# Where the small products of the norms between sub-layers stand in TensorE's order

## The chip, the cores and the metric

One core of one Trainium2 chip runs the whole program. The metric is the device time of one execution in microseconds; of several executions the median is given.

## What is computed

One inference step of a hybrid backbone: two layers of three sub-layers each, on 512 latent and 128 context tokens of width 1024. A sub-layer is wrapped in two RMS norms:

```python
def rms_norm(x, gain):
    x32 = x.astype(F32)
    y = x32 * lax.rsqrt(jnp.mean(x32 * x32, axis=-1, keepdims=True) + RMS_EPS)
    return y.astype(x.dtype) * gain

def modulated_in(x, gain, m):
    return rms_norm(x, gain) * (1 + m[:, None, 1]) + m[:, None, 0]

def residual_out(x, y, gain, m, weight):
    return x + weight * m[:, None, 2] * rms_norm(y, gain)
```

The input of a sub-layer is `modulated_in(x)`, its output y goes into x by `residual_out`. The sub-layers in order are (0,0) SwiGLU, (0,1) attention together with an RWKV-7 scan, (0,2) SwiGLU, (1,0) SwiGLU, (1,1) a bidirectional S5, (1,2) SwiGLU.

## The kernel before

Everything is kept transposed: 128 channels on the partitions, 640 tokens along the free axis, eight tiles `x[d]` for the 1024 channels. The tokens are worked in two halves of 320 columns, half 0 and half 1. Each weight block of 128 columns is loaded by a DMA (`w`), split by `wsplit` (L402) into a high part `whi` (a cast on ScalarE, ACT) and a low part `wlo` (a subtraction on VectorE, DVE, or now and then on GpSimd, POOL), and the activations are split alike into `hh` and `hl`. A product of a block is `mm3` (L431): for each of the eight (or more) tiles of the contraction three matmuls of 128x320, lines L440, L441 and L442. In what follows "a product" is one call of `mm3`, "a matmul" one instruction.

The last stage of a sub-layer goes through its output blocks for half 0, then for half 1. Each block is copied out (y), squared on ACT (L373) and added up on POOL (ssy, L374). When the last block of a half is out, `on_half` (L2072) is called. It runs this chain, with x in place:

- `rms_bcast` of ssy (L326): three matmuls of one column, `ps_ms` (L333); add of the epsilon on DVE (L336); the power on POOL (`rr`, L337); three `diag` on DVE (L341); three matmuls `ps_rb` that spread the factors over all partitions (L342). `ps_ms` and `ps_rb` are the small products that this document is about.
- `post_norm` (L382): per tile, yr = y times factors on DVE (L391), x += yr on DVE (L394), then the square on ACT (L373) and its add on POOL (`ssx`, L374).
- `rms_bcast` of ssx, and `pre_norm` (L345) for the next sub-layer: xr on DVE (L355), `hh` on ACT (L357), `hl` on DVE (L358).

For half 0 the chain runs while PE works on half 1's blocks. For half 1 the post-norm is emitted at once, with the first weights of the next sub-layer ahead of it (`early_weights`, L416); its second part, from ssx on, is kept in `pending` and emitted by `flush` (L444) after the next sub-layer's first products of half 0, in `ab` at L783, in `s5` at L1889. The next sub-layer does its first blocks for half 0, then the same for half 1, then goes on block by block.

The order on each engine is not the order of the code: a scheduler places the instructions by their dependences, their priorities and an estimate of their times; `issue_after` bars an instruction from standing ahead of another one. Within an engine the order that it wrote is kept on the chip, so that an instruction that waits holds up all that stand behind it on its engine.

Of the kernel before, what the change touches and what calls it, by code (L numbers as in the profile page):

```python
# [17 lines left out]
KT = D // 128  # L18
# [14 lines left out]
class K:  # L33


    def __init__(self, ctx, tc, I, O):
        self.ctx, self.tc, self.nc, self.I, self.O = ctx, tc, tc.nc, I, O
        self.pools, self.last, self.last_load = {}, [None] * 3, None
        self.const = self.open("const", 1)
        self.dram = self.open("dram", 1, space=bass.MemoryType.DRAM)  # L40

# [71 lines left out]
    def setup(self):  # L113
# [107 lines left out]
        for t in range(4):  # L221
            self.ada_piece(0, 0, 1, t, pre[4 + t])
        self.first_norm = self.pre_norm(0, 0, 0, rb)
        self.pending = lambda: self.pre_norm(0, 0, 1, self.rms_bcast(ss))
        self.close("boot")
        self.boot = None

# [96 lines left out]
            self.nc.sync.dma_start(dst, xo)  # L324


    def rms_bcast(self, ss):

        nc = self.nc
        ps = self.ps("ps_ms", "pn")  # L330

        for i, c in enumerate((0, 128, 192)):
            nc.tensor.matmul(ps[:, i:i + 1], ss[:, c:c + 128], self.mean, start=True, stop=True)  # L333
        ms = self.small.tile([128, 4], F32, name="ms")
        r = self.small.tile([128, 4], F32, name="rr")
        nc.vector.tensor_scalar(ms[:, :3], ps[:, :3], 1e-6, None, op0=OP.add)  # L336
        self.last_norm = nc.gpsimd.tensor_tensor(r[:, :3], ms[:, :3], self.mhalf[:, :3], op=OP.pow)  # L337
        rb = self.ps("ps_rb", "pn")
        dg = self.small.tile([128, HALF], F32, name="diag")
        for i, (p, c, n) in enumerate(((0, 0, 128), (0, 128, 128), (64, 256, 64))):  # L340
            nc.vector.tensor_scalar(dg[p:, c:c + n], self.ident[p:, p:], r[p:, i:i + 1], None, op0=OP.mult)  # L341
            nc.tensor.matmul(rb[:, c:c + n], self.ones[p:, :], dg[p:, c:c + n], start=True, stop=True)  # L342
        return rb

    def pre_norm(self, l, j, half, rb):  # L345
# [33 lines left out]
            self.sq_add(ss, self.x[d][:, half * HALF:(half + 1) * HALF], d == 0)  # L379
        return ss  # L380

    def post_norm(self, l, j, half, y, ssy, stats=True):  # L382

        nc = self.nc
        m = self.mods[l, j]
        rb = self.rms_bcast(ssy)
        ss = self.small.tile([128, HALF], F32, name="ssx", bufs=2) if stats else None
        for d in range(KT):
            t = self.small.tile([128, HALF], F32, name="yr", tag="n320", bufs=4)
            for a, b, g in SEGS[half]:  # L390
                nc.vector.scalar_tensor_tensor(t[:, a:b], y[d][half][:, a:b], m[:, 2, d, g:g + 1], rb[:, a:b],  # L391
                                               op0=OP.mult, op1=OP.mult)
            xs = self.x[d][:, half * HALF:(half + 1) * HALF]
            nc.vector.tensor_tensor(xs, xs, t, op=OP.add)  # L394
            if stats:
                self.sq_add(ss, xs, d == 0)
        return ss
# [35 lines left out]
    def mm3(self, ps, whl, acts, half, kt, k0=0, k1=None):  # L433

        nc = self.nc
        hi, lo = whl
        ah, al = acts
        o = ps[:, :HALF]
        for k in range(k0, k1 or kt):
            nc.tensor.matmul(o, hi[:, k], ah[k][half], start=(k == 0), stop=False)  # L440
            nc.tensor.matmul(o, hi[:, k], al[k][half], start=False, stop=False)  # L441
            self.last[0] = nc.tensor.matmul(o, lo[:, k], ah[k][half], start=False, stop=(k == kt - 1))  # L442

    def flush(self):  # L444

        if self.pending:
            with ExitStack() as c:
                for i in self.last:
                    c.enter_context(self.tc.issue_after(i.ins))
                self.pending()  # L450
        self.pending = None


# [276 lines left out]
    def ab(self, l, j, on_half, fillers):  # L730
# [36 lines left out]
        def weights(kind, n, eng=None):  # L767
            if self.early[1]:
                return self.early[1].pop(0)
            if kind == "q":  # L770
                return q_weights(n)
            return in_weights({"rw": 768 + n * 128, "k": 512, "v": 640}[kind], eng)

        def one(item, half, w):
            ps = self.ps("ps_in")
            self.mm3(ps, w, acts, half, KT)
            self.ab_take(*item, half, ps)


        for n in range(ahead):  # L780
            one(seq[n], 0, weights(*seq[n], nc.gpsimd if n in (4, 6) else None))
        nxt = [weights(*seq[n]) for n in range(3)]
        self.flush()  # L783
        self.ab_setup()
        for n in range(ahead):
            one(seq[n], 1, nxt.pop(0) if nxt else weights(*seq[n]))
# [947 lines left out]
    def s5(self, l, j, on_half, fillers):  # L1734
# [150 lines left out]
        for d in range(KT):  # L1885
            if d in (4, 6):
                in_load(d // 2)
            proj(d, 0, in_weights(d))
        self.flush()  # L1889
        ws = []  # L1890
        rows = self.t320("s5_s0r")[:, :128]
        self.load(rows, I["state_s5"][0, 0].rearrange("d r (p h) n -> (d r p) (h n)", h=2))
# [166 lines left out]
    def run(self, subs):  # L2059
# [7 lines left out]
        for n, (l, j) in enumerate(order):  # L2067
# [2 lines left out]
            nxt = order[n + 1] if n + 1 < len(order) else None  # L2070

            def on_half(half, y, ssy):  # L2072
                if half and nxt:
                    self.early_weights(*nxt)
                ss = self.post_norm(l, j, half, y, ssy, nxt is not None)
                if nxt and half == 0:
                    self.new_h()
                    self.pre_norm(*nxt, 0, self.rms_bcast(ss))
                elif nxt:
                    self.pending = lambda to=nxt, ss=ss: self.pre_norm(*to, 1, self.rms_bcast(ss))  # L2080

            fill = ([late] if n == 0 else []) + self.ada(l, j, (2,))
            if nxt:
# [73 lines left out]
```

## Time and profile before

| what | value |
|---|---|
| median of 3 executions | 3195.02 us (3191.65 to 3197.65) |
| the profiled execution | 3184.59 us |
| its span | 3182.8 us |
| PE busy | 2900.1 us (91%), 22675 matmuls |
| DVE, ACT, POOL busy | 2080.4 us (65%), 1267.9 us (40%), 954.2 us (30%) |
| mean granted clock | 0.942 of full speed |

The profile is one execution. PE is TensorE. "Idle before" an instruction is the time in which its engine stood still ahead of it, with what ended that time behind the arrow. The granted clock of a stretch is given as a share of 2.4 GHz. A matmul's length overlaps with its neighbours, so that its cost is read from start to start.

### The profile page before, as it was taken

To read this page: it belongs to the slowest core of one execution; us is meant where nothing else is said; L and a number is where in the kernel's file an instruction comes from. 1 tells how busy PE (TensorE), PEld (TensorE's weight loads), DVE (VectorE), ACT (ScalarE), POOL (GpSimd) and SP (SyncE) were. 2 spreads that over 40 slices of the span, in tenths; PEclk is the share of its full clock that TensorE was granted. 3 is DMA by queue.
4 is the path that set the end of the run, shared out by engine and by line. 5 is a ranking of instruction groups with operands and counts; after the bars stand their busy time and mean duration, and the time that the engine had idled before them with its cause. 6 is when DMAs were issued, how large, how long until landed. Compare 5 with 4: busy or idle time off the path is not lost. (4 is left out here: it accounts for less than half of the span.)

```text
span 3182.8 us, 57458 instructions
## 1 busy us (share of the span) xinstructions
PE 2900.1 (91%) x22675; PEld 2704.9 (85%) x22675; DVE 2080.4 (65%) x4199; ACT 1267.9 (40%) x2675; POOL 954.2 (30%) x1010
## 2 busy tenths in 40 slices
PE   6999998987788788999999999999986689999997
PEld 5999998875566567999999999999985589989997
DVE  4876687524746654864675885665777945976776
ACT  4533345423444434533333552332452235533343
POOL 2322235114312201533241322232223633332332
PEclk8999998987888888999999999999997889999998
DMA  6434325631111107354453455453468753442223
GB/s 248 139 120 133 121 89 189 206 133 49 22 33 31 26 15 204 100 171 130 152 157 118 150 153 164 138 163 105 151 149 213 275 177 113 146 146 83 90 71 116
DMA packets 367411, 412.76 MB, mean 130 GB/s; under 512 B 75433, under 2 KB 332262, under 8 KB 366630
## 3 DMA queue, kind: packets, MB, share of 16 engines
q1 hardware_dynamic: 351270, 359.64, 36.8%
q0 software_dynamic: 15872, 49.45, 5.1%
q8 instruction: 179, 2.93, 0.4%
q14 instruction: 90, 0.74, 0.1%
HBM read 357.74 MB, written 50.10 MB: 128 GB/s over the span
## 5 line engine op out<-in xcount | busy, mean ns | idle before, releaser
L413 DVE TENSOR_TENSOR wlo<-w,whi 128x1024 fp32r<-128x1024 f32 (+3 forms) x486 | 472.4, 979 | 265.0 <-ACT whi L412 259.2
L412 ACT CAST whi<-w 128x1024 fp32r<-128x1024 f32 (+3 forms) x488 | 394.4, 817 | 572.7 <-PE ps_y L441 189.7
L440 PE MATMUL ps_h<-hh,whi 128*128 128x320 f32 x1248 | 390.4, 314 | 4.8 <-ACT hh L357 2.4
L441 PE MATMUL ps_h<-hl,whi 128*128 128x320 f32 x1248 | 390.5, 313 | 0.7 <-DVE hl L358 0.7
L442 PE MATMUL ps_h<-hh,wlo 128*128 128x320 f32 x1248 | 389.0, 312 | 0.1
L442 PE MATMUL ps_y<-gh,wlo 128*128 128x320 f32 x1056 | 327.2, 312 | 1.5 <-DVE wlo L413 1.2
L441 PE MATMUL ps_y<-gl,whi 128*128 128x320 f32 x1056 | 327.5, 312 | 0.0
L440 PE MATMUL ps_y<-gh,whi 128*128 128x320 f32 x1056 | 323.8, 314 | 2.6 <-ACT whi L412 1.4
L440 PEld LDWEIGHTS ps_h<-hh,whi 128*128 128x128 f32 x1248 | 236.5, 190 | 9.0 <-issue 3.0
L441 PEld LDWEIGHTS ps_h<-hl,whi 128*128 128x128 f32 x1248 | 236.2, 189 | 5.4 <-issue 3.5
L442 PEld LDWEIGHTS ps_h<-hh,wlo 128*128 128x128 f32 x1248 | 236.1, 189 | 2.6 <-issue 2.0
L440 PEld LDWEIGHTS ps_y<-gh,whi 128*128 128x128 f32 x1056 | 198.1, 189 | 7.9 <-issue 2.5
L442 PEld LDWEIGHTS ps_y<-gh,wlo 128*128 128x128 f32 x1056 | 199.1, 189 | 4.5 <-DVE wlo L413 2.7
L503 DVE TENSOR_TENSOR wlo<-w,whi 128x512 fp32r<-128x512 f32 x216 | 181.8, 867 | 31.7 <-ACT whi L502 30.8
L441 PEld LDWEIGHTS ps_y<-gl,whi 128*128 128x128 f32 x1056 | 199.6, 189 | 1.7 <-issue 1.3
L502 ACT CAST whi<-w 128x512 fp32r<-128x512 f32 x216 | 128.0, 619 | 154.6 <-POOL w L517 47.6
L440 PE MATMUL ps_wide<-hh,whi 128*128 128x320 f32 x576 | 182.3, 317 | 2.5 <-ACT hh L357 1.3
L441 PE MATMUL ps_wide<-hl,whi 128*128 128x320 f32 x576 | 181.4, 315 | 0.4 <-DVE hl L358 0.4
L442 PE MATMUL ps_wide<-hh,wlo 128*128 128x320 f32 x576 | 180.6, 314 | 0.0
L718 DVE TENSOR_TENSOR y<-y,ps_y 128x320 f32<-128x320 f32 x228 | 108.8, 483 | 88.4 <-PE ps_y L442 87.7
L374 POOL TENSOR_TENSOR ssy<-ssy,sq 128x320 f32<-128x320 f32 x84 | 88.6, 1055 | 204.1 <-ACT sq L373 201.2
L374 POOL TENSOR_TENSOR ssx<-ssx,sq 128x320 f32<-128x320 f32 x84 | 102.7, 1224 | 125.7 <-ACT sq L373 121.9
(583 smaller groups left out, 7864.7 us busy)
## 6 DMA issues: line engine op xcount, KB each, us to landing
w<-in_ffn_w_dram SPq DMA_DIRECT2D x112, 1024.0 KB
ada_w<-in_ada_w_dram SPq DMA_DIRECT2D x72, 1024.0 KB
w<-in_ffn_w_dram SPq DMA_DIRECT2D x104, 512.0 KB
w<-in_ab_w_in_dram SPq DMA_DIRECT2D x14, 1024.0 KB
xd<-x POOLq DMA_DIRECT2D x4, 2560.0 KB, 10.8
s5cd<-s_work POOLq DMA_DIRECT2D x128, 64.0 KB, 2.4
s5bd<-s_st POOLq DMA_DIRECT2D x32, 256.0 KB, 4.3
s5bt<-s5bd SPq DMA_DIRECT2D x32, 256.0 KB
```

What stands on the lines that cost most here:

```text
L374: nc.gpsimd.tensor_tensor(ss, ss, sq, op=OP.add)
L412: a = self.nc.scalar.copy(hi[:, :kt], s)
L413: v = (eng or self.nc.vector).tensor_tensor(lo[:, :kt], s, hi[:, :kt].bitcast(F32), op=OP.subtract)
L440: nc.tensor.matmul(o, hi[:, k], ah[k][half], start=(k == 0), stop=False)
L441: nc.tensor.matmul(o, hi[:, k], al[k][half], start=False, stop=False)
L442: self.last[0] = nc.tensor.matmul(o, lo[:, k], ah[k][half], start=False, stop=(k == kt - 1))
L502: nc.scalar.copy(h, src)
L503: v = nc.vector.tensor_tensor(l, src, h.bitcast(F32), op=OP.subtract)
L718: nc.vector.tensor_tensor(yt, yt, ps[:, :HALF], op=OP.add)
```

## The change

`rms_bcast` is cut in two, `rms_stat` (from ps_ms to rr) and `rms_rows` (diag and ps_rb). Half 0's chain is no longer emitted at once: `later(n, step)` puts a step on a list, and `tick`, called at the end of each product, counts down and emits it, with `issue_after` that product's last matmul. So of half 1's eight products the second is followed by ps_ms of ssy, the third by ps_rb and the post-norm, the seventh by ps_ms of ssx, the eighth by ps_rb and the pre-norm. Of half 1's chain the post-norm's small products are held: manual dependences put ps_ms behind the first and ps_rb behind the second product of the next sub-layer. `flush` emits only ps_ms of ssx, and ps_rb with the pre-norm comes one product later; in `ab` and `s5` the call of `flush` goes one product forward for that. The number of instructions on each engine stays as it was, and SP's queue, which issues the loads, keeps its order.

```diff
--- before.py
+++ after.py
@@ -36,6 +36,8 @@
     def __init__(self, ctx, tc, I, O):
         self.ctx, self.tc, self.nc, self.I, self.O = ctx, tc, tc.nc, I, O
         self.pools, self.last, self.last_load = {}, [None] * 3, None
+
+        self.todo, self.hold, self.pending = [], [], None
         self.const = self.open("const", 1)
         self.dram = self.open("dram", 1, space=bass.MemoryType.DRAM)
 
@@ -221,7 +223,7 @@
         for t in range(4):
             self.ada_piece(0, 0, 1, t, pre[4 + t])
         self.first_norm = self.pre_norm(0, 0, 0, rb)
-        self.pending = lambda: self.pre_norm(0, 0, 1, self.rms_bcast(ss))
+        self.pending = ss, lambda rb: self.pre_norm(0, 0, 1, rb)
         self.close("boot")
         self.boot = None
 
@@ -324,22 +326,54 @@
             self.nc.sync.dma_start(dst, xo)
 
 
+    def later(self, n, step):
+
+        self.todo.append([n, step])
+
+    def tick(self):
+
+        for i in self.hold.pop(0) if self.hold else ():
+            self.tc.add_manual_dep(
+                i, self.last[0].ins.name,
+                mybir.DependencyInfo(mybir.DependencyClass.NoSync, mybir.DependencyReason.DATA),
+                reason="norm behind a product")
+        if self.todo:
+            self.todo[0][0] -= 1
+            if self.todo[0][0] <= 0:
+                with self.tc.issue_after(self.last[0].ins):
+                    self.todo.pop(0)[1]()
+
+    def drain(self):
+        while self.todo:
+            self.todo.pop(0)[1]()
+
     def rms_bcast(self, ss):
+        return self.rms_rows(self.rms_stat(ss))
+
+    def rms_stat(self, ss):
 
         nc = self.nc
         ps = self.ps("ps_ms", "pn")
+        self.small_products = [[], []]
 
         for i, c in enumerate((0, 128, 192)):
-            nc.tensor.matmul(ps[:, i:i + 1], ss[:, c:c + 128], self.mean, start=True, stop=True)
+            self.small_products[0].append(
+                nc.tensor.matmul(ps[:, i:i + 1], ss[:, c:c + 128], self.mean, start=True, stop=True).ins)
         ms = self.small.tile([128, 4], F32, name="ms")
         r = self.small.tile([128, 4], F32, name="rr")
         nc.vector.tensor_scalar(ms[:, :3], ps[:, :3], 1e-6, None, op0=OP.add)
         self.last_norm = nc.gpsimd.tensor_tensor(r[:, :3], ms[:, :3], self.mhalf[:, :3], op=OP.pow)
+        return r
+
+    def rms_rows(self, r):
+
+        nc = self.nc
         rb = self.ps("ps_rb", "pn")
         dg = self.small.tile([128, HALF], F32, name="diag")
         for i, (p, c, n) in enumerate(((0, 0, 128), (0, 128, 128), (64, 256, 64))):
             nc.vector.tensor_scalar(dg[p:, c:c + n], self.ident[p:, p:], r[p:, i:i + 1], None, op0=OP.mult)
-            nc.tensor.matmul(rb[:, c:c + n], self.ones[p:, :], dg[p:, c:c + n], start=True, stop=True)
+            self.small_products[1].append(
+                nc.tensor.matmul(rb[:, c:c + n], self.ones[p:, :], dg[p:, c:c + n], start=True, stop=True).ins)
         return rb
 
     def pre_norm(self, l, j, half, rb):
@@ -379,11 +413,10 @@
             self.sq_add(ss, self.x[d][:, half * HALF:(half + 1) * HALF], d == 0)
         return ss
 
-    def post_norm(self, l, j, half, y, ssy, stats=True):
+    def post_norm(self, l, j, half, y, rb, stats=True):
 
         nc = self.nc
         m = self.mods[l, j]
-        rb = self.rms_bcast(ssy)
         ss = self.small.tile([128, HALF], F32, name="ssx", bufs=2) if stats else None
         for d in range(KT):
             t = self.small.tile([128, HALF], F32, name="yr", tag="n320", bufs=4)
@@ -440,6 +473,8 @@
             nc.tensor.matmul(o, hi[:, k], ah[k][half], start=(k == 0), stop=False)
             nc.tensor.matmul(o, hi[:, k], al[k][half], start=False, stop=False)
             self.last[0] = nc.tensor.matmul(o, lo[:, k], ah[k][half], start=False, stop=(k == kt - 1))
+        if (k1 or kt) == kt:
+            self.tick()
 
     def flush(self):
 
@@ -447,7 +482,9 @@
             with ExitStack() as c:
                 for i in self.last:
                     c.enter_context(self.tc.issue_after(i.ins))
-                self.pending()
+                ss, norm = self.pending
+                stat = self.rms_stat(ss)
+            self.later(1, lambda: norm(self.rms_rows(stat)))
         self.pending = None
 
 
@@ -779,8 +816,10 @@
 
         for n in range(ahead):
             one(seq[n], 0, weights(*seq[n], nc.gpsimd if n in (4, 6) else None))
+            if n == ahead - 2:
+                self.flush()
+        self.drain()
         nxt = [weights(*seq[n]) for n in range(3)]
-        self.flush()
         self.ab_setup()
         for n in range(ahead):
             one(seq[n], 1, nxt.pop(0) if nxt else weights(*seq[n]))
@@ -1886,7 +1925,9 @@
             if d in (4, 6):
                 in_load(d // 2)
             proj(d, 0, in_weights(d))
-        self.flush()
+            if d == KT - 2:
+                self.flush()
+        self.drain()
         ws = []
         rows = self.t320("s5_s0r")[:, :128]
         self.load(rows, I["state_s5"][0, 0].rearrange("d r (p h) n -> (d r p) (h n)", h=2))
@@ -2070,14 +2111,30 @@
             nxt = order[n + 1] if n + 1 < len(order) else None
 
             def on_half(half, y, ssy):
-                if half and nxt:
-                    self.early_weights(*nxt)
-                ss = self.post_norm(l, j, half, y, ssy, nxt is not None)
-                if nxt and half == 0:
+                if half:
+
+                    self.drain()
+                    if nxt:
+                        self.early_weights(*nxt)
+                    ss = self.post_norm(l, j, 1, y, self.rms_bcast(ssy), nxt is not None)
+                    if nxt:
+                        self.hold = self.small_products
+                        self.pending = ss, lambda rb, to=nxt: self.pre_norm(*to, 1, rb)
+                    return
+                box = {}
+
+                def post():
+                    box["ss"] = self.post_norm(l, j, 0, y, self.rms_rows(box["r"]), nxt is not None)
+
+                def pre():
                     self.new_h()
-                    self.pre_norm(*nxt, 0, self.rms_bcast(ss))
-                elif nxt:
-                    self.pending = lambda to=nxt, ss=ss: self.pre_norm(*to, 1, self.rms_bcast(ss))
+                    self.pre_norm(*nxt, 0, self.rms_rows(box["s"]))
+
+                self.later(2, lambda: box.update(r=self.rms_stat(ssy)))
+                self.later(1, post)
+                if nxt:
+                    self.later(4, lambda: box.update(s=self.rms_stat(box["ss"])))
+                    self.later(1, pre)
 
             fill = ([late] if n == 0 else []) + self.ada(l, j, (2,))
             if nxt:
```

The order on PE from the end of (0,0) on. Here ps_wide<-gh is the last product of (0,0), ssx and ssy are the sums of squares (ssy_4908 is half 1's), ps_in and ps_wide<-hh are products of (0,1), hh_0 of half 0 and hh_1 of half 1. Before:

```order
L442 MATMUL ps_wide<-gh,wlo 128x320
L333 MATMUL ps_ms<-mean,ssx 128x1 x3
L342 MATMUL ps_rb<-diag,ones 128x128 x2
L342 MATMUL ps_rb<-diag,ones 128x64
L333 MATMUL ps_ms<-mean,ssy_4908 128x1 x3
L440 MATMUL ps_in<-hh_0_5378,whi 128x320 x3
...
L342 MATMUL ps_rb<-diag,ones 128x128 x2
L342 MATMUL ps_rb<-diag,ones 128x64
...
L333 MATMUL ps_ms<-mean,ssx 128x1 x3
L342 MATMUL ps_rb<-diag,ones 128x128 x2
L342 MATMUL ps_rb<-diag,ones 128x64
L440 MATMUL ps_wide<-hh_1_5379,whi 128x320
```

And with the change:

```order
L475 MATMUL ps_wide<-gh,wlo 128x320
L361 MATMUL ps_ms<-mean,ssx 128x1 x3
L376 MATMUL ps_rb<-diag,ones 128x128 x2
L376 MATMUL ps_rb<-diag,ones 128x64
L473 MATMUL ps_in<-hh_0_5602,whi 128x320 x3
...
L361 MATMUL ps_ms<-mean,ssy_4908 128x1 x3
...
L376 MATMUL ps_rb<-diag,ones 128x128 x2
L376 MATMUL ps_rb<-diag,ones 128x64
...
L361 MATMUL ps_ms<-mean,ssx 128x1 x3
...
L376 MATMUL ps_rb<-diag,ones 128x128 x2
L376 MATMUL ps_rb<-diag,ones 128x64
L473 MATMUL ps_wide<-hh_1_5603,whi 128x320
```

The three products of ssy_4908 moved from ahead of the first product of (0,1) to 52 matmuls later; ps_rb moved from 32 matmuls after the start of half 0 to 82; ps_ms of ssx moved from directly ahead of the next ps_rb to one product (24 matmuls) ahead of it. So 62 matmuls stand between ps_rb and ps_ms of ssx, where 136 stood.

The order on DVE at (0,2) to (1,0): diag and xr belong to half 1's pre-norm, hl_1_18622 and hl_1_18889 are its first tile's low part, s_work is background work for the later S5. Before:

```order
L341 TENSOR_SCALAR diag<-ident,rr 64x64
L413 TENSOR_TENSOR wlo<-w,whi 128x512 x2
...
L1694 TENSOR_TENSOR s_work<-s_bc,s_lp 128x2x16x8
L1695 TENSOR_TENSOR s_work<-s_bc,s_lp 128x2x16x8
L355 SCALAR_TENSOR_TENSOR xr<-x,mods_13285,ps_rb 128x192
...
L355 SCALAR_TENSOR_TENSOR xr<-x,mods_13285,ps_rb 128x128
L413 TENSOR_TENSOR wlo<-w,whi 128x1024
L1678 TENSOR_TENSOR s_work<-s_work 128x256 x2
L1696 TENSOR_TENSOR s_work<-s_work 128x256
L358 SCALAR_TENSOR_TENSOR hl_1_18622<-xr,mods_13285,hh_1_18606 128x192
```

And with the change:

```order
L374 TENSOR_SCALAR diag<-ident,rr 64x64
L446 TENSOR_TENSOR wlo<-w,whi 128x512
L446 TENSOR_TENSOR wlo<-w,whi 128x1024
L389 SCALAR_TENSOR_TENSOR xr<-x,mods_13285,ps_rb 128x192
...
L389 SCALAR_TENSOR_TENSOR xr<-x,mods_13285,ps_rb 128x128
L1715 TENSOR_TENSOR s_work<-s_bc,s_lp 128x256
...
L1734 TENSOR_TENSOR s_work<-s_bc,s_lp 128x2x16x8
L446 TENSOR_TENSOR wlo<-w,whi 128x1024 x2
L392 SCALAR_TENSOR_TENSOR hl_1_18889<-xr,mods_13285,hh_1_18873 128x192
```

Six s_work stood ahead of the first xr, and one wlo and three more s_work between the last of the eight xr and the first hl; now those six stand, with two wlo, between the last xr and the first hl.

Counts of 128x320 matmuls at the other places, read from the same orders:

| place | before | with the change |
|---|---|---|
| (0,0) to (0,1): matmuls by which half 0's first ps_ms is later |  | 36 |
| (0,1) to (0,2): the same |  | 8 to 9 |
| (0,1) to (0,2): from ps_rb of half 1's pre-norm to half 1's first product | 101 | 48 |
| (0,2) to (1,0): the same | 36 | 16 |
| (1,0) to (1,1): matmuls by which half 1's ps_rb of the post-norm is later |  | 14 |
| (1,1) to (1,2): matmuls by which half 0's ps_rb of the post-norm is later |  | 11 |
| (1,1) to (1,2): the same | 80 | 36 |

On POOL at the end of (0,0), four adds of half 1's ssy stood between half 0's last ssx add and the power of its pre-norm; with the change one stands ahead of the ssx adds and two behind them.

## Rows read from the trace of the kernel before

**Rows 1.** Waits of PE, whole span: total us, times, longest.

```profile
PE ps_rb L342 <- DVE diag L341: 20.7, 7, 6.0
PE ps_ms L333 <- POOL ssy L374: 11.7, 4, 3.9
PE ps_ms L333 <- POOL ssx L374: 6.8, 3, 3.9
```

**Rows 2.** Windows: length, busy us (count) of PE, PEld, DVE, ACT, POOL, granted clock, DMA.

```profile
491.40:498.20 6.80, 5.42 (x20) 5.14 (x21) 3.67 (x7) 3.13 (x4) 2.12 (x3) 0.50 1.01 322
sum 90.40, PE 63.51 PEld 58.23 DVE 63.31 ACT 32.42 POOL 20.97; mean PE 7.06 PEld 6.47 DVE 7.03 ACT 3.60 POOL 2.33
```

**Rows 3.** PE's timeline, end of (0,0): start, length, instruction, [idle before it <- releaser].

```profile
492.78 1.44 PE L333 MATMUL ps_ms<-mean,ssy 128*128 128x1 f32 x6 [3.92 <-POOL ssy L374]
494.19 0.64 PE L440 MATMUL ps_y<-gh,whi 128*128 128x320 f32 x1
495.89 0.47 PE L440 MATMUL ps_y<-gh,whi 128*128 128x320 f32 x1
...
498.02 0.40 PE L442 MATMUL ps_y<-gh,wlo 128*128 128x320 f32 x1
...
501.46 0.31 PE L442 MATMUL ps_y<-gh,wlo 128*128 128x320 f32 x1
...
502.93 0.31 PE L440 MATMUL ps_y<-gh,whi 128*128 128x320 f32 x1
```

**Rows 4.** ACT's timeline, end of (0,0) and of the last sub-layer.

```profile
493.30 1.56 ACT L412 CAST whi<-w 128x768 fp32r<-128x768 f32 x2 [2.88 <-DMA w<-in_ffn_w_dram]
...
3135.01 1.56 ACT L412 CAST whi<-w 128x768 fp32r<-128x768 f32 x2 [4.24 <-DMA w<-in_ffn_w_dram]
```

**Rows 5.** PE's timeline, (0,1) to (0,2), and (1,1) to (1,2).

```profile
1263.74 1.01 PE L333 MATMUL ps_ms<-mean,ssy 128*128 128x1 f32 x4 [3.18 <-POOL ssy L374]
...
1295.30 1.81 PE L342 MATMUL ps_rb<-diag,ones 128*128 128x128 f32 x6 [3.98 <-DVE diag L341]
...
2694.53 1.84 PE L342 MATMUL ps_rb<-diag,ones 128*128 128x128 f32 x6 [3.78 <-DVE diag L341]
```

**Rows 6.** PE's timeline, start of (0,1).

```profile
525.06 1.81 PE L342 MATMUL ps_rb<-diag,ones 128*128 128x128 f32 x6 [6.00 <-DVE diag L341]
534.90 0.97 PE L342 MATMUL ps_rb<-diag,ones 128*128 128x128 f32 x6
...
557.35 0.83 PE L333 MATMUL ps_ms<-mean,ssx 128*128 128x1 f32 x6 [1.35 <-POOL ssx L374]
```

**Rows 7.** DVE's timeline in the last sub-layer: the last x of half 0.

```profile
3153.32 1.16 DVE L394 TENSOR_TENSOR x<-x,yr 128x320 f32<-128x320 f32 x1
```

**Rows 8.** POOL's lines, 539.4 to 557.4 us: total and mean ns | idle before.

```profile
L374 POOL TENSOR_TENSOR ssx<-ssx,sq 128x320 f32<-128x320 f32 x7 | 11.9, 1698 | 0.3
L413 POOL TENSOR_TENSOR wlo<-w,whi 128x1024 fp32r<-128x1024 f32 x2 | 5.2, 2606 | 8.4 <-ACT whi L412 8.4
L301 POOL DMA_DIRECT2D xd<-x x1 | 0.6, 612 | 0.0
```

**Rows 9.** PE's timeline, (0,2) to (1,0).

```profile
1847.09 0.43 PE L342 MATMUL ps_rb<-diag,ones 64*128 64x64 f32 x2
1854.14 0.41 PE L440 MATMUL ps_wide<-hh,whi 128*128 128x320 f32 x1 [1.12 <-ACT y L716]
1855.08 0.41 PE L441 MATMUL ps_h<-hl,whi 128*128 128x320 f32 x1 [0.31 <-DVE hl L358]
```

**Rows 10.** DVE's timeline, (0,2) to (1,0).

```profile
1847.04 0.42 DVE L1676 TENSOR_TENSOR s_work<-s_bc,s_lp 128x256 f32<-128x256 f32 x1 [0.41 <-DMA s_bc<-s5bc]
...
1849.88 2.41 DVE L355 SCALAR_TENSOR_TENSOR xr<-x,mods,ps_rb 128x192 f32<-128x192 f32 x8
1852.19 1.23 DVE L413 TENSOR_TENSOR wlo<-w,whi 128x1024 fp32r<-128x1024 f32 x1
```

**Rows 11.** PE's timeline, (1,0) to (1,1).

```profile
2359.25 1.44 PE L333 MATMUL ps_ms<-mean,ssx 128*128 128x1 f32 x6 [3.90 <-POOL ssx L374]
```

## The prediction

> **What bounds the kernel now.** TensorE (PE) is the busiest engine by far (the table above), so time is won only where PE stands still or is clocked down. I read its waits first: ps_rb behind the DVE's diag 20.7 us, ps_ms behind POOL's ssy adds 11.7, ps_ms behind its ssx adds 6.8 [rows 1]; together 39.2 us. Then the granted clock of the stretches behind these waits: nine of them, 90.4 us in all, at 0.50, that is 1.2 GHz, with PE busy for 63.5 us [rows 2]. One matmul of 128x320 takes 0.267 us there (eight from 495.89 to 498.02) and 0.147 at 2.4 GHz (ten from 501.46 to 502.93 [rows 3]), so at most half of the 63.5 us, 32 us, lies in the clock. The upper bound of the whole idea is thus 39 + 32 = 71 us. The question is which of these waits end on something that the change moves.
>
> **What goes at the first wait of a boundary.** At (0,0) to (0,1) PE idles 3.92 us for ssy and issues its next real product at 494.19 [rows 3]. That product needs a whi, whose cast ACT starts at 493.30, after a wait for the DMA of w_ffn; two casts take 1.56 us, so the first is done near 494.1 [rows 4]. With the small product out of the way PE would have idled until the same 494.19. The end of the last sub-layer reads alike: ACT waits 4.24 us for a DMA there and starts the cast at 3135.01 [rows 4]. SP's queue keeps its order, so both are costed at 0 gained; were the load earlier, 3.9 each would be won. At (0,1) to (0,2) the ssy wait is 3.18 us [rows 5]; nine matmuls more ahead of it fill 9 x 0.147 = 1.3 of it. But half 0's chain (yr, x, eight squares, seven adds on POOL, pow, diag) starts no earlier, and it sets the later wait of 3.98 us [rows 5]: I take -1.2 (-2.5 to +1).
>
> **What is late next, half 0.** Elsewhere a chain starts later. In (0,0) to (0,1) ps_ms goes 36 matmuls back: from 494.19, at half clock until 498.2, they end near 501.3, and with 33 more ps_rb stands near 506, where it is soon after 500 now. Six us later start yr and x. The second ps_rb has waited 6.00 us until 525.06 [rows 6]. In POOL's old order four adds of the other half stood ahead of this chain's pow; now three do. I cost it at +1.2 (0 if the chain has all the slack, +3 if half of the six arrives). At (1,1) to (1,2) the rows part moves 11 matmuls = 1.6 us back, and the 3.78 us wait [rows 5] hangs on that chain: +1.6 (0 to +3). At the end x of half 0 was complete at 3154.5 [rows 7], and comes about 6 later, near the time at which PE reads it: +0.5 (0 to +1.5).
>
> **Half 1, whose post-norm is now held behind the next sub-layer's products.** This is the larger part.
> (a) (0,0) to (0,1): ps_ms of ssy goes 52 matmuls back. PE starts on ps_in at 526.9 without it, 20 matmuls at half clock until 532.3 and 65 at full, so ps_rb moves from 534.90 to 542. ps_ms of ssx, though, stands 24 matmuls *earlier* than before, since flush went one product forward: 62 matmuls lie between the two, 136 before. From ps_rb to ssx it took 557.35 - 534.90 = 22.4 us, of which PE waited 1.35 [rows 6]. POOL was full for the last 18: seven adds 11.9, two wlo 5.2, a spill 0.6 [rows 8]. In the new order the two wlo stand together ahead of the adds, which I take to save some 7 us of the 22.4, their own 5.2 and some waiting for squares; so the last add is still at about 557.5, while PE arrives at 542 + 0.9 + 62 x 0.147 = 552. A new wait of 5 to 6 us, then 24 matmuls at half clock (6.4 us) ahead of ps_rb, which were done by then before: ps_rb at 564.8 for 561.08. Half 1 starts 2 to 6.5 us later: +3.5.
> A page speaks against this place too. The Trainium skill (SBUF — State Buffer, section Who interferes with whom) says that a DVE instruction with two SBUF inputs and a GpSimd one that reads SBUF exclude each other. The seven adds took 1.70 us each [rows 8], and wlo and x += yr on the DVE are of that kind. By that rule each add that newly meets a wlo could lose up to the DVE's 1.2 us; the sum goes by the row, which holds such meetings already.
> (b) (0,1) to (0,2): 48 matmuls are left between ps_rb and half 1, before 101. 48 x 0.147 = 7.1 us cover the xr, hh and hl work of the first tiles with little to spare: +1 (0 to +2).
> (c) (0,2) to (1,0): 16 matmuls are left, before 36: 2.4 us of cover. Before, ps_rb's last product started at 1847.09, PE got its first hl at 1855.08, and waited 1.12 and 0.31 us [rows 9]. In the new DVE order eight xr, six s_work and two wlo stand in between: 2.4 + 6 x 0.4 + 2 x 1.2 = 7.2 us [rows 10]. So the first hl is about 7.5 us behind ps_rb, when PE has 2.4 us of ps_y and 0.6 of hh products to do. A new wait of 4 to 5 us, and, as behind the 3.98 us one [rows 5], a stretch at 1.2 GHz, of which 10 us cost up to 5; against that stand the old waits of 1.4 us, and the rest of the DVE's work is no longer in the way afterwards. Together +4.5 (+2 to +8).
> (d) (1,0) to (1,1): ps_rb goes 14 matmuls = 2.1 us back, ps_ms of ssx stays; the 3.90 us wait [rows 11] grows by what the DVE cannot catch up, about one wlo of 1.2 us [rows 10]: +1 (0 to +2.5).
> (e) (1,1) to (1,2): 36 matmuls are left, before some 80: 5.3 us of cover, just short: +0.5 (0 to +2).
>
> **Sum.** -1.2 + 1.2 + 1.6 + 0.5 + 3.5 + 1 + 4.5 + 1 + 0.5 = 12.6 us. PE issues as many instructions as before. The profiled execution took 3184.59 us and would take about 3197.2; it stands 10.4 us under the median of the runs, 3195.02, and on that basis the forecast is 3207.6 us. The ends add up to +1.5 and +29.5, which needs all terms at one end at once. A measurement of this kernel tells 0.2%, 6.4 us, from no change.
>
> **Rivals.**
> 1. *The waits go: faster.* For it: 39 us of waits name just these tiles [rows 1], and half 0's small products do get a place behind work. One mechanism: the DMA of w lands earlier than now, so that the three waits of 3.92, about 3.9 and 3.18 us go (11 us) together with the slow stretches behind them. The first of those holds 5.42 us of PE work at half clock [rows 2], so 2.7 us each, 8 in all: -19. It decides once that load is over 3 us sooner after the last gh than now; against it, ACT waits for the DMA and not for PE [rows 4]. With half of my costs left, -19 + 6 = -13: 3182 us. Chance 0.14.
> 2. *No change.* The chains catch up in the slack that the waits of 6.00, 3.98 and 3.78 us give them, and (a) and (c) come out at their low ends: 2 + 2, the others cancel: +4, 3199 us, between 3189 and 3201. Chance 0.20.
> 3. *The clock alone: no change by another way.* PE stood still for 3.92 and 3.98 us ahead of stretches at 0.50, and ran on at full speed after the 1.12 us of [rows 9]. If the waits only move and come out shorter, three slow stretches go though the idle time stays: -8 us of clock against my +12.6, 3200 us. The Trainium skill (TensorE: Matmul & The Clock Gate, section Why this matters for your kernels) has it that idle gaps between bursts drop the rate and dense work keeps it, and by that rule the new places would pay. The trace agrees on the drop; whether the new waits are shorter no row shows, and (a) and (c) say no. Chance 0.08.
> 4. *Slower, my forecast.* Chance 0.58, its own range 3202 to 3224.
> That the order does not change is excluded by the moved rows on PE.
>
> **Numbers.** 3207.6 us; the range 3188 to 3223 leaves out most of the faster case and the slow tail, about 2 in 10. Faster 0.14; within 0.2%: 0.28, of rivals 2 and 3; slower 0.58.
>
> **What would show it.** Right: no wait for ps_ms behind ssy at the first boundary and at the end, but one as long of ps_y for whi; a new wait of 5 us for ps_ms behind ssx in (0,1) and of 3 us or more for ps_h behind hl in (1,0), each with a clock of 0.50 behind it. Wrong: PE's idle time at these boundaries down by over 10 us, no half clock near 494 or 3135, or hl in time in (1,0).

## The result and the profile after

The changed kernel takes 3211.78 us (median of 5 runs, 3206.34 to 3216.49), the kernel before 3191.65 us in the same comparison (5 runs, 3186.41 to 3197.65). The ratio is 1.0055 (1.0041 to 1.0069): about 17.5 us (13 to 22) slower.

The page of the kernel after, first lines:

```profile
span 3204.6 us, 57429 instructions
...
PE 2903.9 (91%) x22675; PEld 2709.4 (85%) x22675; DVE 2085.4 (65%) x4199; ACT 1268.8 (40%) x2675; POOL 954.6 (30%) x1010
```

PE's busy time was 2900.1 us in a span of 3182.8 and is 2903.9 in 3204.6: of the 21.8 us between the two profiled executions (4 more than by the ratio, since one execution each is compared) only 3.8 are busy time, the slower clock included; 18.0 are idle. What PE waited for in the kernel after, over the whole span, columns as in [rows 1]:

```profile
PE ps_hb L1064 <- ACT xb L1060: 20.3, 10, 4.6
...
PE ps_rb L376 <- DVE diag L374: 16.3, 5, 5.5
...
PE ps_ms L361 <- POOL ssx L408: 12.4, 3, 5.3
PE ps_y L473 <- ACT whi L445: 11.2, 2, 5.6
...
PE ps_in L473 <- ACT pm L994: 6.2, 1, 6.2
...
PE ps_h L473 <- ACT hh L391: 5.8, 3, 2.4
...
PE ps_ms L361 <- POOL ssy L408: 2.8, 2, 2.1
```

The same groups in the kernel before; for pm it has none:

```profile
PE ps_hb L1025 <- ACT xb L1021: 15.1, 9, 4.6
...
PE ps_h L440 <- ACT hh L357: 2.4, 1, 2.4
...
PE ps_y L440 <- ACT whi L412: 1.4, 1, 1.4
```

The three groups of [rows 1] fell from 39.2 to 31.5 us, ssy's alone from 11.7 to 2.8. In their place stand waits for whi (1.4 before, now 11.2), for pm (none before), for hh at ps_h (2.4, now 5.8) and for xb at ps_hb (15.1 in 9, now 20.3 in 10): 7.7 us won, 24.6 lost. The small products wait less, and what stands behind them waits more.

To place the 21.8 us I paired the same PSUM evictions of both traces and took the median shift of their starts within each sub-layer; the difference from one to the next is what the boundary between them cost. In us (e1 to e10 are the experiments below), beside the terms of the prediction for that place:

| place | predicted | change | e1 half 0 | e2 half 1 | e4 old flush | e5 pad | e6 no last hold | e10 control |
|---|---|---|---|---|---|---|---|---|
| up to the end of (0,0) | 0 | 1.5 | -1.2 | 2.0 | -0.1 | -0.2 | -0.4 | -0.7 |
| (0,0) to (0,1) | 4.7 | 8.9 | 3.8 | 5.2 | 9.3 | 4.7 | 8.2 | 0.8 |
| inside (0,1) | 0 | 5.0 | 2.7 | 4.8 | -6.1 | -6.9 | 2.9 | 0.2 |
| (0,1) to (0,2) | -0.2 | -1.5 | 1.6 | 1.1 | -0.6 | -0.9 | -0.9 | 0.5 |
| (0,2) to (1,0) | 4.5 | -0.4 | 2.7 | -0.1 | 2.0 | -0.6 | -0.6 | 2.3 |
| (1,0) to (1,1) | 1.0 | 0.9 | -0.6 | 0.8 | 1.9 | 2.2 | 0.5 | -1.4 |
| inside (1,1) | 0 | 0.2 | 1.7 | 1.1 | -0.5 | -0.9 | 1.0 | -1.6 |
| (1,1) to (1,2) | 2.1 | 7.1 | 4.4 | 7.5 | 7.2 | 6.3 | 2.7 | 0.4 |
| end | 0.5 | 0.2 | 0.9 | -0.5 | 0.8 | 0.9 | 1.1 | -0.7 |

The control has before's order, profiled again: two profiles of one order differ by up to 2.3 us at a place, so a smaller step tells little. Each column is one execution against the one of before, so that its steps need not add up to the ratio of the runs: e2's add up to 21.9 us, where its ratio (below) gives 13. Steps of the other experiments are named where they are used.

**The first wait of a boundary** changed its name and kept its length. PE's and ACT's timelines of the kernel after, (0,0) to (0,1), columns as in [rows 3]:

```profile
495.87 0.64 PE L473 MATMUL ps_y<-gh,whi 128*128 128x320 f32 x1 [5.57 <-ACT whi L445]
...
494.98 1.56 ACT L445 CAST whi<-w 128x768 fp32r<-128x768 f32 x2 [3.12 <-DMA w<-in_ffn_w_dram]
```

At 492.78 PE waited 3.92 us for ssy [rows 3]; the small product stands elsewhere now, and PE waits 5.57 us for the whi that ACT could cast only when its DMA was in, as in [rows 4]. That product started at 494.19 [rows 3]; 495.87 is 1.7 later, 1.5 of which (0,0) had lost. The end reads alike (PE waits 5.60 us for whi until 3156.46).

**The new wait in (0,1).** PE, ACT and DVE at ps_in of (0,1), kernel after:

```profile
525.96 1.44 PE L361 MATMUL ps_ms<-mean,ssx 128*128 128x1 f32 x6 [5.30 <-POOL ssx L408]
529.60 0.77 PE L376 MATMUL ps_rb<-diag,ones 128*128 128x128 f32 x2 [2.20 <-DVE diag L374]
...
532.65 0.64 PE L473 MATMUL ps_in<-hh,whi 128*128 128x320 f32 x1 [1.23 <-ACT hh L391]
...
556.97 0.63 PE L473 MATMUL ps_in<-hh,whi 128*128 128x320 f32 x1 [6.23 <-ACT pm L994]
...
565.90 0.72 PE L361 MATMUL ps_ms<-mean,ssx 128*128 128x1 f32 x6
...
556.06 0.43 ACT L993 COPY praw<-ps_in 128x320 f32<-128x320 f32 x1 [2.94 <-DVE yr L424]
556.38 0.53 ACT L994 ACTIVATE pm<-ps_in,derived 128x320 f32<-128x320 f32 x1
...
553.61 2.42 DVE L424 SCALAR_TENSOR_TENSOR yr<-y,mods,ps_rb 128x192 f32<-128x192 f32 x8
```

Half 0's 6.00 us wait [rows 6] became 5.30 + 2.20 + 1.23. Then comes a wait that no row of before has: 6.23 us at 556.97 for pm. PE wants a free PSUM bank; the bank is emptied by the ACT copy to praw and the pm behind it; and the copy stood still for 2.94 us, until 556.06, for a yr of the DVE. The yr at 553.61 (eight, 2.42 us) ends at about the same time. The copy reads nothing of the DVE's: praw and pm come from pools that are opened for (0,1) in SBUF that y of (0,0) held. By the program's addresses the first praw lies on y's last tile; the last reader of that tile is half 1's post-norm, which the hold has moved behind products of (0,1). The ps_ms of ssx, where I had put the wait, starts at 565.90 without one.

**The DVE at (1,1) to (1,2).** What the DVE waited for there, kernel before (2690 to 2790 us) and after (2704.5 to 2809.4 us):

```profile
DVE wlo L413 <- ACT whi L412: 3.3, 2, 3.0
DVE diag L341 <- POOL rr L337: 2.4, 1, 2.4
DVE g L621 <- PE ps_h L442: 1.7, 1, 1.7
```

```profile
DVE ms L364 <- PE ps_ms L361: 7.1, 3, 4.1
DVE xr L389 <- PE ps_rb L376: 2.7, 2, 1.5
DVE wlo L446 <- ACT whi L445: 2.3, 3, 1.2
DVE diag L374 <- POOL rr L365: 1.6, 1, 1.6
...
2723.98 0.16 DVE L364 TENSOR_SCALAR ms<-ps_ms 128x3 f32<-128x3 f32 x1 [4.06 <-PE ps_ms L361]
```

In the kernel before the DVE is busy for some 92 of the 100 us there. Its queue keeps its order, and the ms of a held ps_ms now stands in it ahead of other work: 7.1 us of waiting that was not there, 4.06 of them in one piece.

### The profile page after: what moved, and what is told of

It is laid out like the page before. It is cut to its first block, busy times and chain, and to the rows that moved or that the text cites. A ratio compares the mean times of both kernels' runs of the same rounds, so it can differ in the third digit from the quotient of the medians.

```text
span 3204.6 us, 57429 instructions
## 1 busy us (share of the span) xinstructions
PE 2903.9 (91%) x22675; PEld 2709.4 (85%) x22675; DVE 2085.4 (65%) x4199; ACT 1268.8 (40%) x2675; POOL 954.6 (30%) x1010
## 4 chain that ended last, share of the span: by engine, by line
PE 73%; DVE 11%; DMA 5%; POOL 3%; issue 3%; ACT 2%; SPq 1%; POOLq 0%; DVEq 0%; ACTq 0%
PE ps_h L474 6%; PE ps_h L473 6%; PE ps_h L475 6%; PE ps_y L473 5%; PE ps_y L474 5%; PE ps_y L475 5%; PE ps_wide L473 4%; PE ps_wide L474 4%; PE ps_wide L475 4%; DMA w<-in_ffn_w_dram 2%; PE ps_wide L277 2%; PE ps_z L571 1%; PE ps_z L573 1%; PE ps_z L572 1%; PE ps_in L473 1%
## 5 line engine op out<-in xcount | busy, mean ns | idle before, releaser
L473 PE MATMUL ps_y<-gh,whi 128*128 128x320 f32 x1056 | 324.6, 315 | 12.1 <-ACT whi L445 11.2
L473 PEld LDWEIGHTS ps_h<-hh,whi 128*128 128x128 f32 x1248 | 237.0, 190 | 12.6 <-ACT hh L391 6.5
L473 PEld LDWEIGHTS ps_y<-gh,whi 128*128 128x128 f32 x1056 | 198.6, 190 | 17.3 <-ACT whi L445 12.6
```

## The experiments

**One half at a time.** e1 keeps half 0's places and puts half 1 back; the calls of flush stand behind their loops again.

```diff
-                        self.hold = self.small_products
...
-                stat = self.rms_stat(ss)
-            self.later(1, lambda: norm(self.rms_rows(stat)))
+                norm(self.rms_bcast(ss))
```

> Half 0's chain is placed as in the change; half 1's post-norm and flush stand as before. My theory, that holding half 1's post-norm costs the time: within 6 us of the kernel before, at the first boundary about +1 to +3 us, and from 2700 to 2830 us no loss. Rival, that half 0's later chain is the cost: +12 to +20 us, nearly the whole loss.

e2 does the reverse, with half 0's products where they stood before.

```diff
-                self.later(2, lambda: box.update(r=self.rms_stat(ssy)))
-                self.later(1, post)
+                ss = self.post_norm(l, j, 0, y, self.rms_bcast(ssy), nxt is not None)
...
-                    self.later(4, lambda: box.update(s=self.rms_stat(box["ss"])))
-                    self.later(1, pre)
+                    self.new_h()
+                    self.pre_norm(*nxt, 0, self.rms_bcast(ss))
```

> Half 0's chain is emitted at once as before; half 1's hold and the moved flush stay. My theory: +12 to +20 us against before, with PE's wait of about 6 us for pm near 557 us and the loss of about 7 us between 2700 and 2830 us both there. Rival (half 0 is the cost): within 6 us of before.

Both came out at 1.0041 (1.0027 to 1.0054, and 1.0027 to 1.0056), 13 us each where the whole has 17.5. That half 0 alone stays near the time of before is refuted. At (0,0) to (0,1) the halves add up (3.8 + 5.2 for 8.9). At (1,1) to (1,2) they don't (4.4 + 7.5 for 7.1), and inside (0,1) both lose. PE's wait for pm is 1.77 us in e1 and 6.23 in e2: it belongs to half 1.

**The hold and flush apart.** e3 is the change without the hold, the first line of e1's diff alone. e4 is the change with flush as before, the rest of that diff:

```diff
-                stat = self.rms_stat(ss)
-            self.later(1, lambda: norm(self.rms_rows(stat)))
+                norm(self.rms_bcast(ss))
```

> The change without the hold alone: half 1's post-norm products stand directly at the boundary, flush stays one product forward with its rows one product later. If the hold is the cost: 0 to +6 us against before, no wait for pm in (0,1). If the moved flush is the cost (a ps_ms that stands a product too early): +8 us or more, with PE waiting some 6 us for ps_ms of half 1's ssx near 550 us.

> The change with flush at its old place, both products together, and the hold kept. If the hold is the cost: +12 to +20 us, the wait for pm near 557 us as long as in the change. If the moved flush is the cost: 0 to +6 us and no such wait.

e3 1.0046 (1.0026 to 1.0065), e4 1.0030 (1.0019 to 1.0041). PE's longest wait for pm, one timeline row each, e3 and then e4:

```profile
551.61 0.55 PE L473 MATMUL ps_in<-hh,whi 128*128 128x320 f32 x1 [1.78 <-ACT pm L994]
```

```profile
555.28 0.64 PE L473 MATMUL ps_in<-hh,whi 128*128 128x320 f32 x1 [6.24 <-ACT pm L992]
```

Without the hold 1.78, with it 6.24, whichever place flush has: the hold makes the wait. (0,0) to (0,1) costs 5.8 in e3 and 9.3 in e4; (1,1) to (1,2) 1.9 and 7.2. Against the change (8.9 and 7.1), e3 lacks only the hold: at the two places it costs 3.1 and 5.2 us. With flush as before, e4 against e1, it costs 5.5 and 2.8, so that how it divides between them is not settled. The whole times of both missed what I expected (+14.7 us for 0 to +6, and +9.6 for +12 to +20): besides the 5.8, e3 loses 4.5 inside (0,1), where e4 wins 6.1 (below).

**The memory.** e5 is the change with 6.8 KB of each partition kept empty, so that praw doesn't lie on y.

```diff
+        self.open("pad").tile([128, 1744], F32, name="pad")
...
-        self.close("mixh", "mixg", "act", "whl", "wraw", "small")
+        self.close("mixh", "mixg", "pad", "act", "whl", "wraw", "small")
```

> The change, with 6.8 KB per partition left empty ahead of praw and pm, so that praw no longer lies where y lay; in the program's order its first copy on ACT then has no wait on the DVE. If that reuse of y's memory makes PE wait 6.23 us for pm in (0,1): that wait falls to under 1.5 us there and the first boundary costs +3 to +5 us in place of +8.9; the rest as in the change, in all some 4 us less than the change. If the wait comes from ACT's queue or from banks alone: 5 us or more remain.

1.0022 (1.0013 to 1.0031). The same places on PE and ACT in e5:

```profile
555.34 0.41 PE L473 MATMUL ps_in<-hh,whi 128*128 128x320 f32 x1 [1.80 <-ACT pm L995]
...
542.74 0.42 ACT L994 COPY praw<-ps_in 128x320 f32<-128x320 f32 x1
```

In the program's order the first praw copy waits for PE alone now, where it waited for the DVE; it follows its cast at 542.74, PE's wait falls from 6.23 to 1.80, and the boundary from 8.9 to 4.7. Only addresses were changed by hand, so this cause is shown. I had expected under 1.5 us. The pm of the first two blocks come from another pool and still lie on y's first tiles; ACT takes them behind the pm of 554.75 for which PE waits, and until then two PSUM banks of ps_in stay full. Whether the 1.80 us come of that no run shows. Of the 10.5 us by which e5's ratio is better than the change's, the boundary has 4.2; inside (0,1) e5 wins 6.9 where the change loses 5.0.

**The last hold.** e6 is the change without the hold at (1,1); e11 has that and e5's empty memory.

```diff
-                        self.hold = self.small_products
+                        if (l, j) != (1, 1):
+                            self.hold = self.small_products
```

> The change without the hold at (1,1) to (1,2) alone. If the DVE, which waits there 7.1 us in all for ps_ms, loses these as it has no slack up to 2790 us: the loss between 2690 and 2850 us falls from +7.1 to +2 to +4, with DVE waits for ps_ms under 3 us. If half 0's later chain makes the loss there: it stays +6 or more.

> The change with both remedies: the memory left empty as in e5 and no hold at (1,1) to (1,2) as in e6. If the two costs of the hold are these two: about +4 to +5 us at the first boundary, +2 to +3 between 2690 and 2850 us, and with the order of e5 near 930 us 0 to +5 us against before in all, 2 to 6 us less than e5. If they overlap with something else: as long as e5 or longer.

e6 1.0051 (1.0037 to 1.0064), not to be told from the change by the total; e11 1.0008 (0.9999 to 1.0018), against e5's 1.0022. The DVE's waits of e6, 2700 to 2805 us:

```profile
DVE wlo L446 <- ACT whi L445: 3.7, 3, 2.2
DVE xr L389 <- PE ps_rb L376: 3.4, 2, 2.0
DVE diag L374 <- POOL rr L365: 2.6, 2, 1.6
DVE ms L364 <- PE ps_ms L361: 1.2, 2, 0.8
```

ms waits 1.2 us for 7.1, and the boundary costs 2.7 for 7.1. e11 against e5 points the same way: 3.7 us less at this boundary in the table's measure (2.6 against 6.3), and by the ratios 4.4 in all (2.6 against 7.0 over before), though the two intervals overlap. e11's first boundary costs 4.2.

**Half 0, one product earlier.** e9 is e1 with ps_ms of ssy behind one product, not two, and that of ssx behind five, not four.

```diff
-                self.later(2, lambda: box.update(r=self.rms_stat(ssy)))
+                self.later(1, lambda: box.update(r=self.rms_stat(ssy)))
...
-                    self.later(4, lambda: box.update(s=self.rms_stat(box["ss"])))
+                    self.later(5, lambda: box.update(s=self.rms_stat(box["ss"])))
```

> e1 with ps_ms of half 0's ssy behind the first product of half 1 in place of the second. If half 0's cost at the first boundary is the late start of its chain, it falls from +3.8 to between 0 and +2 us, and at the other boundaries the places are those of before, so that they cost 0 (+-1) in place of +1.6, +2.7 and +4.4. If it is the queues' new order and not the start: +3 or more at the first boundary. It also has the order of e8 near 930 us, so that its total is no measure of this.

1.0002 (0.9993 to 1.0012). (0,0) to (0,1) still costs 3.0, against 3.8 in e1 and 0.8 in the control, so the place of ps_ms is not shown to be the reason for half 0's cost there. (1,1) to (1,2) fell from 4.4 to 0.3.

**The other way to help half 0.** On the kernel before: POOL's adds of the other half stand behind half 0's power (e7), and with the empty memory too (e12). The edit is in sq_add; self.rr0 is the power of half 0's pre-norm.

```diff
-            nc.gpsimd.tensor_tensor(ss, ss, sq, op=OP.add)
+            a = nc.gpsimd.tensor_tensor(ss, ss, sq, op=OP.add)
+            if self.rr0:
+                self.tc.add_manual_dep(
+                    a.ins, self.rr0, mybir.DependencyInfo(mybir.DependencyClass.NoSync, mybir.DependencyReason.DATA),
...
```

> Not the change: the kernel before, with POOL's adds of half 1's ssy put behind the power of half 0's second norm by order alone. Four or five adds of 0.9 us stood ahead of that power at three boundaries, where PE waited 6.00, 3.98 and 3.78 us. If POOL's queue sets those waits: each falls by 2 to 4 us, one or two slow stretches go, -6 to -14 us against before. If the adds or squares themselves set them, or half 1's chain gives it back: within 5 us of before.

> e7 with the empty memory of e5. In e7 PE waited 2.57 us for pm in (0,1) after the earlier second norm. If y's memory is what it waited for: under 1.5 us there and 1 to 4 us less than e7 in all, -5 to -9 us against before. If not: as e7, -2 to -5 us.

0.9987 (0.9978 to 0.9996) and 0.9986 (0.9977 to 0.9995): 4 us faster than before, the only two that are. The reason is not the one I had. In e7:

```profile
522.52 0.77 PE L343 MATMUL ps_rb<-diag,ones 128*128 128x128 f32 x2 [3.74 <-DVE diag L342]
...
547.78 0.42 PE L445 MATMUL ps_in<-hh,whi 128*128 128x320 f32 x1 [2.57 <-ACT pm L960]
```

The rb waits fell as expected (6.00 to 3.74 here, 3.98 to 1.39 and 3.78 to 1.19 at the other two), yet the three boundaries cost 0.2, -0.3 and 2.0: half 1's chain gave the gain back, here in a wait of 2.57 us for pm. e12 takes that away, and PE waits 2.57 us for ssx at 557.34 instead, so that e12 is as long as e7 and not 1 to 4 us shorter. The 4 us come from inside (0,1): -6.3 and -5.2.

**Inside (0,1).** In e4, e5, e7, e9, e11 and e12 another order stands there: kk_sq, an ACT instruction that waits for the load of rw_k, comes behind four uv copies that it stood ahead of. e8 forces it on the kernel before, by placing the loads of a state and of rw_r, which stand ahead of rw_k's in SP's queue, behind the last att_out store; e10 is the control, the change with all three parts undone.

```diff
-            nc.sync.dma_start(self.od[i][:, qb * 128:(qb + 1) * 128], o)
+            self.od_last = nc.sync.dma_start(self.od[i][:, qb * 128:(qb + 1) * 128], o).ins.name
...
+        if i == 1:
+            self.last_load, keep = self.od_last, self.last_load
```

> Not the change: the kernel before, with one store of att_out put ahead of the load of a state and of rw_r in SP's queue near 930 us, by order alone; e4, e5 and e7 have that order and spent some 10 us less between 920 and 1050 us than the change. If that order is worth it: -4 to -11 us against before, all of it between 920 and 1050 us. If those kernels got it by something else: within 3 us of before.

> The change's code with all three parts undone: every engine's order is that of before. It shows how far two profiles of one order differ: 0 (+-0.5) us at the boundaries; between 660 and 1250 us 0 if the +4.0 us of the change there is the change's, +3 to +5 if the profile of before was a quick one there.

e10 took 3185.02 us in one run, before 3184.58. e8 0.9992 (0.9982 to 1.0001) does not settle it. PE in the kernel before, and in e8:

```profile
938.21 0.63 PE L1279 MATMUL ps_v<-ident,v_rev 128*64 128x128 f32 x2 [5.28 <-ACT uv L1281]
```

```profile
941.12 0.61 PE L1006 MATMUL ps_hs<-k_hsel,kk_sq 128*128 128x2 f32 x4 [2.34 <-ACT kk_sq L1177]
```

The 5.28 us wait gives way to one of 2.34, but e8 loses some 3 us again later in (0,1), and (0,1) to (0,2) costs it 3.2. Its profiled execution took 3192.06 us where the median of its runs is 3182.97, so its single places say little. The six kernels win where that order stands; that the order alone is worth 4 us is not shown.

The change's own loss in there, 5.0, is another pair. ACT, before and after:

```profile
996.54 0.40 ACT L1021 COPY xb<-gn_r 128x256 f32<-128x256 f32 x1 [1.74 <-PE ps_hb L1025]
998.66 0.83 ACT L1177 ACTIVATE kk_sq<-rw_k,col_c 128x640 f32<-128x640 f32 x1 [1.72 <-DMA rw_k<-rwd]
```

```profile
1011.92 0.83 ACT L1216 ACTIVATE kk_sq<-rw_k,col_c 128x640 f32<-128x640 f32 x1 [3.83 <-DMA rw_k<-rwd]
1012.66 0.39 ACT L1060 COPY xb<-gn_r 128x256 f32<-128x256 f32 x1
...
1013.10 1.22 PE L1064 MATMUL ps_hb<-ident,xb 128*128 128x128 f32 x4 [3.50 <-ACT xb L1060]
```

Before, xb went first, and then kk_sq with its wait for rw_k. In the changed kernel kk_sq is ahead, waits 3.83 us, and xb and PE's ps_hb wait with it. But e2 has before's order of the two and loses 4.8 in (0,1), so this pair is a part of the cause at most. The rest stays open.

## Why the prediction was right, and where it was not

The direction, the rival chosen and the reason (the waits move on to what stands behind the small products, and the chain behind them starts later) held. The two largest terms did not hold as reasoned: (a) came by another mechanism, (c) came and cost nothing. The forecast of +12.6 us met +17.5, by terms that erred both ways; that it lies so near is in part luck, since the 4.5 us of (c) did not come and 5.0 came inside (0,1), where I had put nothing. Of the signs named ahead, the wait for whi came at the first boundary and at the end; the waits for ssx in (0,1) and for hl in (1,0) did not, and hl in time in (1,0) was named as a sign of being wrong.

- **First waits, 0 gained:** right, at (0,0) and at the end; whi and its DMA took the place of ssy. Rival 1 fell with it: the load came no earlier. PE idles there for 5.6 us instead of 3.9, and the product behind stands where it stood.
- **(0,1) to (0,2), -1.2 and (b) +1:** measured -1.5. PE's wait for ssy fell from 3.18 to 2.06, that for rb rose from 3.98 to 5.49.
- **Half 0 at (0,0), +1.2 (0 to 3):** mis-sized. e1 has 3.8, with 0.8 in the control; e2 with e1 makes up the 8.9, so it does not come from the other half. Three waits (5.30, 2.20, 1.23) stand where I had one.
- **(a), +3.5:** size nearly right (5.2 in e2), the wait too (6.23 us against 5 to 6), the mechanism wrong. That the size agrees is luck: I put the wait at ps_ms behind POOL's ssx; it is the praw copy behind y's last reader, and I had looked at the engines' queues and not at who had the memory before. The seven adds took 1.02 us each for 1.70 in [rows 8]. POOL's line of the kernel after, 552 to 563.5 us, then single rows of POOL and DVE, two of before and three of after:

```profile
L408 POOL TENSOR_TENSOR ssx<-ssx,sq 128x320 f32<-128x320 f32 x7 | 7.1, 1018 | 2.9 <-ACT sq L407 2.5
...
548.17 1.98 DVE L413 TENSOR_TENSOR wlo<-w,whi 128x1024 fp32r<-128x1024 f32 x1 [3.16 <-ACT whi L412]
549.03 1.85 POOL L374 TENSOR_TENSOR ssx<-ssx,sq 128x320 f32<-128x320 f32 x1
...
552.48 1.22 DVE L446 TENSOR_TENSOR wlo<-w,whi 128x1024 fp32r<-128x1024 f32 x1
552.48 1.93 POOL L408 TENSOR_TENSOR ssx<-ssx,sq 128x320 f32<-128x320 f32 x1 [1.68 <-ACT sq L407]
...
560.54 0.87 POOL L408 TENSOR_TENSOR ssx<-ssx,sq 128x320 f32<-128x320 f32 x1
```

Before, four of the seven ran beside a wlo or an x += yr of the DVE and took 1.85 to 3.57 us, the other three 0.86 to 0.89; after, the one that starts with a wlo took 1.93, the others 0.86 to 0.88. The rule that the prediction cites from the Trainium skill (SBUF — State Buffer, Who interferes with whom) agrees with these rows. It cost nothing here because the new order brought fewer such meetings, not more.
- **(c), +4.5:** the wait came, 4.0 us in two pieces, behind hh and y and not hl, and cost nothing that can be measured (-0.4; the control has 2.3). PE at (0,2) to (1,0), kernel after, and the clock behind this wait and behind that at (0,1) to (0,2); last, a row of PE in the kernel before:

```profile
1869.22 0.56 PE L473 MATMUL ps_h<-hh,whi 128*128 128x320 f32 x2 [2.16 <-ACT hh L391]
1869.62 0.30 PE L473 MATMUL ps_wide<-hh,whi 128*128 128x320 f32 x1
1871.76 0.64 PE L473 MATMUL ps_h<-hh,whi 128*128 128x320 f32 x1 [1.84 <-ACT y L753]
...
1871.70:1875.00 3.30, 3.24 (x12) 3.16 (x13) 3.30 (x10) 1.03 (x5) 0.49 (x1) 0.50 0.67 203
1308.50:1318.60 10.10, 7.39 (x26) 6.80 (x27) 8.11 (x18) 3.98 (x8) 1.25 (x2) 0.50 0.17 53
...
1875.45 0.41 PE L440 MATMUL ps_h<-hh,whi 128*128 128x320 f32 x1 [1.69 <-DVE th L619]
```

Two waits of 2.16 and 1.84 us with three matmuls between them left a stretch at 0.50 (1.2 GHz) of 3.3 us, where the single 5.49 us one at (0,1) to (0,2) left 10.1. And before had a wait of 1.69 us for the DVE at 1875.45, in the same sub-layer, that is gone; with the 1.12 and 0.31 us of [rows 9] that is 3.1 of the 4.0. The first hl starts at 1871.35, 7.8 us behind ps_rb's start at 1863.55, near the 7.5 that I had read from the DVE's order; what PE stood at first was hh and y. I read it so that the DVE sets the pace there, and a wait of PE ahead of its work is given back behind it; no run tried this place by itself. I had written that the DVE's work is "no longer in the way afterwards" and given that no number.
- **(d), +1:** right; 3.90 [rows 11] became 4.90 us, the step is 0.9.
- **(1,1) to (1,2), half 0 +1.6:** the wait grew by just that, 3.78 [rows 5] to 5.41. **(e), +0.5 (0 to 2):** mis-sized; 7.1 - 1.6 leaves 5.5, and e6 takes away 4.4 of it. I had counted PE's cover (36 matmuls), and not the DVE, which stands still for a ps_ms that the hold has put later. Why e1, without a hold, loses 4.4 here is not explained.
- **End, +0.5:** 0.2.
- **Not forecast:** 5.0 inside (0,1), as far from the diff as can be, partly through the order of two ACT instructions.
- **Rival 3, the clock:** PE's busy time, in which a slower clock shows, rose by 3.8 us, so nothing was won by it on balance. The stretches at 0.50 at the boundaries say the same: twelve of 97.3 us in all with 63.2 us of PE's work, where before had nine, 90.4 and 63.5 [rows 2]. The Trainium skill's rule (TensorE: Matmul & The Clock Gate, Why this matters for your kernels) that gaps drop the rate agrees with the stretches at 0.50 behind the waits of 6.23 us (6.7 us long) and 5.49 us (10.1), but the waits did not go.

## What to carry to other kernels

Before a consumer is moved later, look up which tile it reads last and what is allocated on that memory next: the first writer there inherits the delay. A small product that is held back holds every in-order queue in which its result is read, so the cover must be counted on that engine (here the DVE, busy for 92 of 100 us before) and not on PE alone. A wait on PE is worth what it delays of the engine that sets the pace of that stretch, so price it there, and expect a scheduler to change order far from the edit; judge by boundary, not by total.

## What the runs showed of the chip and its program that I had not expected

An ACT copy waited 2.94 us for a DVE instruction whose result it doesn't use, and PE 6.23 us behind it; 6.8 KB of empty SBUF took 4.4 us off PE's wait. A 4.0 us wait in two pieces left 3.3 us at 1.2 GHz, one of 5.49 us in one piece 10.1. An add on POOL of 0.87 us took 1.85 to 1.94 beside a wlo on the DVE. And two orders of ACT instructions inside (0,1), none touched by the diff, go with steps of -6.9 to +5.0 us there; how much of these is theirs is not shown.
